# RG-LRU branch of a hybrid block: activations ordered by function over the four column blocks

## Chip, core and metric

The kernel runs on one core of a Trainium2 chip. The metric is device time in microseconds (us) of one execution. The engines are named as the profile names them: PE (matrix products; PEld is its loading of weights), DVE (vector), ACT (scalar engine, which evaluates activation functions from a table that it has to load), POOL and SP (which mostly issue transfers here). Each engine works through its own instructions in program order and waits at an instruction whose inputs are not ready.

## What is computed

A transformer-like block over 256 tokens of width 2048: one wide input projection, four branches in parallel (RG-LRU, attention with a forget gate, Mamba-2, RWKV-7), gates and an output projection, a gated feed-forward part and a last gated addition. All of it is fp32. The part that the change touches is the RG-LRU branch, 512 columns wide:

```python
def rg_lru_branch(x, gate_x, conv_w, conv_b, w_r, b_r, w_i, b_i, lam):
    xc = causal_dwconv(x, conv_w, conv_b)
    xb = xc.reshape(Bsz, S, LRU_BLOCKS, LRU_BLOCK)
    r = sigmoid(einsum('bshi,hij->bshj', xb, w_r) + b_r)
    i = sigmoid(einsum('bshi,hij->bshj', xb, w_i) + b_i)
    log_a = -LRU_C * r * softplus(-lam)
    a = exp(log_a)
    u = xc * i * sqrt(-expm1(2.0 * log_a))
    hseq = associative_scan(combine, (a, u))     # h[t] = a[t] * h[t-1] + u[t]
    return hseq * gelu(gate_x)
```

## The kernel before

Activations lie transposed: features on 128 partitions, 256 tokens along the free axis, so the 512 columns of the branch are four tiles of 128x256, the four blocks `j`.

**The large products** (`gemm_fm`). Weights stream from HBM in chunks of 512 KB (`wr`, four buffers), four feature blocks deep and 256 columns wide. Each chunk is split in two fp32r parts: ACT writes the rounded part (`wh`, L214, three buffers), DVE the remainder (`wl`, L215, three buffers). A unit of 256 output columns is four chunks, each used by 16 matmuls: per feature block and per half of the columns one 128x512 with `wh` and one 128x256 with `wl`. Its two accumulators (`pg`) are two of the four PSUM banks of the pool `psG`. After the last matmul ACT copies one half of the bank (L256) and DVE adds the other (L257, shown as L100, the line of the helper), then DVE multiplies by `R`. Only then is the bank free. Banks are handed out in turn; the small logits' product takes a single one, so from there on a unit gets the second bank of one earlier unit and the first of the next: in the changed kernel's numbers `pg_1002` gets the bank of `pg_719`, `pg_1003` that of `pg_720`, `pg_1106` that of `pg_876`.

**The branches** are Python generators (`lru`, `ssd`, `fox`, `rwkv`). After each chunk a `pump` advances the oldest one to its next `yield`, so that small pieces of branch work lie between the chunks of the large products. Matmuls of a branch (`pb`, pool `psB`) are put into PE's order a little behind the large products' current place (`on_pe`, `DELAY`). From these priorities the framework's scheduler then sets one fixed order for each engine; it places the table loads of ACT too.

**The RG-LRU generator** (`lru`, L523) runs during the projections of `z` and the first `xbc` units, some 60 to 145 us into the execution. For each block: the convolution (ACT an Identity with scale and bias, DVE three multiply-adds, L120), one product each for `r` and `i` with a block-diagonal weight into a `pb` bank, two Sigmoids and a Tanh on ACT, a reciprocal on DVE (L124) and a Sqrt on ACT, four small DVE steps, the scan, a Gelu of the gate column `ag`, and a multiplication. Block 0 goes through all of it before block 1 starts. ACT's functions fall in four tables here: Sigmoid with Tanh, Sqrt, Gelu, and the Silu that the `z` columns need in the same stretch.

Of the kernel before, what the change touches and what calls it, by code (L numbers as in the profile page):

```python
# [10 lines left out]
AF = mybir.ActivationFunctionType  # L11
# [74 lines left out]
def body(tc, T, out, dbg=None):  # L86
# [5 lines left out]
    def shape_n(ap):  # L92
        n = 1
        for s in ap.shape[1:]:
            n *= s
        return n

    def tt(o, a, b, op):
        cost[0] += 0.07 + shape_n(o) / 960.0
        V.tensor_tensor(o, a, b, op=op)  # L100

    def mul(o, a, b):
        tt(o, a, b, ALU.mult)
# [7 lines left out]
    def ts(o, a, s1, s2=None, op0=ALU.mult, op1=ALU.add):  # L111
        cost[0] += 0.07 + shape_n(o) / 1500.0
        if s2 is None:
            V.tensor_scalar(o, a, s1, None, op0=op0)
        else:
            V.tensor_scalar(o, a, s1, s2, op0=op0, op1=op1)
# [5 lines left out]
    def recip(o, a):  # L122
        cost[0] += 0.07 + 8 * shape_n(o) / 960.0
        V.reciprocal(o, a)  # L124

    def act(o, i, f, **kw):
        A.activation(o, i, f, **kw)  # L127
# [10 lines left out]
    def mm(o, l, r, start=True, stop=True):  # L138
        on_pe(PE.matmul, o, l, r, start=start, stop=stop)
# [28 lines left out]
    def slot(dt=F32, pool=sp):  # L168
        return pool.tile([P, S], dt, name="sb" if pool is not sp else "s", tag="s")

    def bank():
        return psB.tile([P, 512], F32, name="pb", tag="pb")
# [9 lines left out]
    def bslot(dt=F32):  # L182
        return slot(dt, bp)
# [166 lines left out]
    def softplus(y, o, w):  # L350

        e, z, z2, q, r = w
        act(e, y, AF.Abs)
        act(e, e, AF.Exp, scale=-1.0)
        ts(r, e, 2.0, None, ALU.add)
        recip(z, r)
        mul(z, z, e)
        mul(z2, z, z)
        ts(q, z2, 1.0 / 17)
        for k in range(7, 0, -1):  # L360
            stt(q, q, 1.0 / (2 * k + 1), z2, ALU.add, ALU.mult)
        stt(q, q, 1.0, z, ALU.add, ALU.mult)
        ts(r, y, 0.0, None, ALU.max)
        stt(o, q, 2.0, r, ALU.mult, ALU.add)
# [35 lines left out]
    raw = {"ax": []}  # L400
# [80 lines left out]
    def pc(name, i):  # L481
        return prm[:, po[name] + i:po[name] + i + 1]
# [24 lines left out]
    def finish(j, tiles):  # L507
        ys[j] = tiles
# [6 lines left out]
    def conv4(x, o, wname, nt, i, bias):  # L515
        if bias is not None:
            act(o, x, AF.Identity, scale=pc(wname, 3 * nt + i), bias=bias)
        else:
            ts(o, x, pc(wname, 3 * nt + i))
        for d in range(1, 4):  # L520
            stt(o[:, d:], x[:, :S - d], pc(wname, (3 - d) * nt + i), o[:, d:], ALU.mult, ALU.add)

    def lru():  # L523
        lam = bc_.tile([P, 7, 4], F32, name="lam")
        lo_ = po["lru_lambda"]
        ts(lam[:, 0], prm[:, lo_:lo_ + 4], -1.0)
        softplus(lam[:, 0], lam[:, 6], [lam[:, i] for i in range(1, 6)])
        ts(lam[:, 0], lam[:, 6], 4.0)
        yield
        res = []  # L530
        for j in range(4):
            ax, ag = raw["ax"][j], raw["ag"][j]
            xc = bslot()
            conv4(ax, xc, "lru_conv_w", 4, j, pc("lru_conv_b", j))
            yield
            pt = bank()
            mm(pt[:, :S], lbd[:, 0, j], xc)
            mm(pt[:, S:], lbd[:, 1, j], xc)
            r, i_ = bslot(), bslot()
            act(r, pt[:, :S], AF.Sigmoid, bias=pc("lru_br", j))  # L540
            act(i_, pt[:, S:], AF.Sigmoid, bias=pc("lru_bi", j))
            t = bslot()
            act(t, r, AF.Tanh, scale=lam[:, 0, j:j + 1])
            yield
            q = r
            ts(q, t, 0.5, 0.5, ALU.mult, ALU.add)
            q2 = bslot()
            recip(q2, q)
            act(t, t, AF.Sqrt)
            yield  # L550
            mul(i_, i_, xc)
            mul(t, t, q2)
            ts(q, q2, -1.0, None, ALU.add)
            mul(i_, i_, t)
            yield
            V.tensor_tensor_scan(xc, q, i_, 0.0, op0=ALU.mult, op1=ALU.add)
            cost[0] += 0.6
            act(t, ag, AF.Gelu_apprx_tanh)
            y = bslot()
            mul(y, xc, t)  # L560
            yield
            res.append(y)
            if dbg is not None:
                dbg("ya", j, y)
            yield
        finish(0, res)
# [568 lines left out]
    hook[0] = first_unit  # L1135
    proj("ag", 0, 2)
    launch("a", lru)
    small_logits()
    proj("z", 2, 2)
# [248 lines left out]
```

## Time and profile before

| | |
|---|---|
| median of 3 runs | 1732.07 us (1731.74 to 1732.73) |
| the profiled execution | 1731.33 us, of which the profile's span is 1729.4 us |
| PE busy | 1713.1 us, 99% of the span |
| DVE busy | 1235.8 us, 71% |
| ACT busy | 946.1 us, 55% |
| ACT table loads | 38, 48.8 us in all |

PE's busy share is so high that time can be gained only where PE stands still, some 16 us in the whole span, or where its clock is below full; and time is lost only where a new wait makes it stand still. A table load is an ACT instruction, so it delays whatever ACT does next, among it the `wh` casts and the copies that empty PE's banks.

### The profile page before, as it was taken

Reading aid. Unit: us, or ns where it says so; the run is one execution under the profiler, and the core shown is the slowest. Engines: PE = TensorE matmul, PEld = TensorE weight load, DVE = VectorE, ACT = ScalarE, POOL = GpSimd, SP = SyncE. Lnnn points to the kernel's source line nnn. Section 1 sums busy time; section 2 is a strip of 40 time slices with the busy share of each in tenths; the row PEclk is TensorE's granted clock in tenths of the full one; section 3 lists DMA queues with packets and bytes.
Section 4 is the critical chain, followed back from the end, with each engine's and each line's share of the span. In section 5 each row is a group of like instructions: output and inputs, shape, how many; then the busy total and the mean of one; then the engine's idle time right before and its main releaser. Section 6 shows DMA issues by size and latency. Waiting matters only on the chain.

```text
span 1729.4 us, 29615 instructions
## 1 busy us (share of the span) xinstructions
PE 1713.1 (99%) x11555; PEld 1558.2 (90%) x11555; DVE 1235.8 (71%) x2006; ACT 946.1 (55%) x1426; POOL 92.6 (5%) x155
## 2 busy tenths in 40 slices
PE   8999999999999999999999999999999999999998
PEld 7888888999999999999888888888888888888887
DVE  6888768687789744648778777777777755555676
ACT  6676555556644444545556555555555544444454
POOL 1000000002320100000210000000000000000000
PEclk9999999999999999999999999999999999999999
DMA  9556556556775854665766666666656666666564
GB/s 330 172 170 217 170 175 225 184 179 206 207 213 178 256 159 150 180 185 189 249 209 192 186 193 187 191 189 189 192 188 202 211 208 189 195 193 186 179 217 139
DMA packets 99132, 338.36 MB, mean 196 GB/s; under 512 B 12362, under 2 KB 16624, under 8 KB 98736
## 3 DMA queue, kind: packets, MB, share of 16 engines
q1 hardware_dynamic: 90528, 310.94, 57.6%
q0 software_dynamic: 7456, 21.81, 4.3%
q10 hardware_dynamic: 1008, 3.73, 0.5%
q8 instruction: 90, 1.47, 0.3%
q14 instruction: 50, 0.41, 0.1%
HBM read 326.95 MB, written 9.48 MB: 195 GB/s over the span
## 4 chain that ended last, share of the span: by engine, by line
PE 94%; DVE 2%; DMA 2%; issue 1%; ACT 1%; SPq 0%; DVEq 0%; ACTq 0%
PE pg L132 90%; PE pb L135 4%; DVE wl L215 1%; PE pb L132 1%; DMA wr<-in_w_p_dram 1%; DMA cbr<-in_consts_dram 0%; DVE e L100 0%; DMA d<-in_xT_dram 0%; ACT wh L214 0%; DVE e L930 0%; DMA wr<-in_w_ax_dram 0%; DVE s L100 0%; ACT e L127 0%; DVE sb L100 0%; DVE s L120 0%
## 5 line engine op out<-in xcount | busy, mean ns | idle before, releaser
L132 PE MATMUL pg<-x,wh 128*128 128x512 f32 (+1 forms) x4384 | 1170.9, 339 | 5.5 <-DVE sb L100 5.3
L215 DVE TENSOR_TENSOR wl<-wr,wh 128x1024 fp32r<-128x1024 f32 (+1 forms) x592 | 715.5, 1210 | 408.1 <-ACT wh L214 400.5
L214 ACT CAST wh<-wr 128x1024 fp32r<-128x1024 f32 (+1 forms) x592 | 615.7, 1041 | 648.0 <-PE pg L132 495.9
L132 PE MATMUL pg<-x,wl 128*128 128x256 f32 (+1 forms) x3344 | 918.3, 282 | 3.4 <-DVE wl L215 3.4
L132 PEld LDWEIGHTS pg<-x,wh 128*128 128x128 f32 x4384 | 746.7, 188 | 91.2 <-DVE sb L100 3.1
L132 PEld LDWEIGHTS pg<-x,wl 128*128 128x128 f32 (+1 forms) x3344 | 628.8, 188 | 17.4 <-DVE wl L215 5.4
L132 PE MATMUL pg<-f,wh 128*128 128x512 f32 x704 | 243.2, 390 | 0.0
L132 PE MATMUL pg<-f,wl 128*128 128x256 f32 x704 | 195.8, 282 | 0.0
L132 PEld LDWEIGHTS pg<-f,wh 128*128 128x128 f32 x704 | 131.7, 188 | 26.9
L132 PEld LDWEIGHTS pg<-f,wl 128*128 128x128 f32 x704 | 133.0, 189 | 1.0
L132 PE MATMUL pg<-sb,wh 128*128 128x256 f32 x512 | 94.7, 283 | 0.0
L120 DVE SCALAR_TENSOR_TENSOR s<-s,prm 128x255 f32<-128x255 f32 (+1 forms) x176 | 84.1, 478 | 1.7 <-ACT s L127 1.0
L132 PEld LDWEIGHTS pg<-sb,wh 128*128 128x128 f32 x512 | 79.2, 188 | 0.1
L256 ACT COPY s<-pg 128x256 f32<-128x256 f32 x136 | 49.7, 366 | 45.8 <-PE pg L132 45.8
L132 PE MATMUL pg<-sb,wl 128*128 128x256 f32 x256 | 72.5, 284 | 0.0
L100 DVE TENSOR_TENSOR s<-s 128x256 f32<-128x256 f32 (+1 forms) x172 | 70.5, 419 | 1.6 <-ACT s L127 0.4
L127 ACT ACTIVATE s<-s 128x256 f32<-128x256 f32 x140 | 56.6, 413 | 14.9 <-DVE s L100 14.5
L100 DVE TENSOR_TENSOR s<-s,pg 128x256 f32<-128x256 f32 x136 | 56.1, 414 | 8.3 <-ACT s L256 6.6
L127 ACT ACTIVATE s<-s,prm 128x256 f32<-128x256 f32 x88 | 52.4, 596 | 0.7 <-DVE s L100 0.7
L127 ACT ACT_TABLE_LOAD x38 | 48.8, 1283 | 1.8 <-PEq L1378 1.2
L132 PEld LDWEIGHTS pg<-sb,wl 128*128 128x128 f32 x256 | 48.0, 188 | 0.2
L132 PE MATMUL pg<-d,wh 128*128 128x512 f32 x128 | 45.2, 395 | 0.0
(235 smaller groups left out, 1152.3 us busy)
## 6 DMA issues: line engine op xcount, KB each, us to landing
wr<-in_w_up_dram SPq DMA_DIRECT2D x176, 512.0 KB, 4.2
wr<-in_w_g_dram SPq DMA_DIRECT2D x128, 512.0 KB, 3.6
wr<-in_w_down_dram SPq DMA_DIRECT2D x88, 512.0 KB, 4.0
wr<-in_w_p_dram SPq DMA_DIRECT2D x76, 512.0 KB, 3.7
wr<-in_w_branch_dram SPq DMA_DIRECT2D x32, 512.0 KB, 3.7
wr<-in_w_out_dram SPq DMA_DIRECT2D x32, 512.0 KB, 3.8
wr<-in_w_ple_gate_dram SPq DMA_DIRECT2D x32, 512.0 KB, 4.2
wr<-in_w_v_dram SPq DMA_DIRECT2D x8, 512.0 KB, 4.4
```

Of the source, the lines that this page charges most:

```text
L100: V.tensor_tensor(o, a, b, op=op)
L120: V.scalar_tensor_tensor(o, a, s, b, op0=op0, op1=op1)
L127: A.activation(o, i, f, **kw)
L132: return f(*a, **kw)
L135: f(*a, **kw)
L214: A.copy(wh, wr)
L215: V.tensor_tensor(wl, wr, wh.bitcast(F32), op=ALU.subtract)
L256: A.copy(o, pt[:, S:])
```

## The change

The first loop now does the Gelus of all four gate columns in place, at the start of the generator. The second loop goes through convolution, products, Sigmoids, Tanh and `q` for the four blocks and keeps the tiles. A third loop does reciprocal, Sqrt, the small steps, the scan and the final multiplication for the four blocks. The number of yields is the same.

```diff
         ts(lam[:, 0], lam[:, 6], 4.0)
         yield
-        res = []
+        res, kept = [], []
         for j in range(4):
-            ax, ag = raw["ax"][j], raw["ag"][j]
+            act(raw["ag"][j], raw["ag"][j], AF.Gelu_apprx_tanh)
+        for j in range(4):
+            ax = raw["ax"][j]
             xc = bslot()
             conv4(ax, xc, "lru_conv_w", 4, j, pc("lru_conv_b", j))
             yield
...
             q = r
             ts(q, t, 0.5, 0.5, ALU.mult, ALU.add)
+            kept.append((xc, i_, t, q))
+        for j, (xc, i_, t, q) in enumerate(kept):
             q2 = bslot()
             recip(q2, q)
             act(t, t, AF.Sqrt)
...
             V.tensor_tensor_scan(xc, q, i_, 0.0, op0=ALU.mult, op1=ALU.add)
             cost[0] += 0.6
-            act(t, ag, AF.Gelu_apprx_tanh)
-            y = bslot()
-            mul(y, xc, t)
+            y = raw["ag"][j]
+            mul(y, xc, y)
             yield
```

What the scheduler makes of it, first on ACT. The four Gelus stand together behind one table load, but the Sigmoids and Sqrts of the blocks still alternate: ACT's order holds 35 table loads against 38. In the names, `pb` is a block's product, `pg` a bank of a large product, `wh` the rounded weights, `prm` and `lam` parameters.

**First place: the second unit of `z` has just been multiplied.** ACT before, from the Sqrt of block 0 on (`pg_719` and `pg_720` are the first unit of `z`):

```order
L127 ACT_TABLE_LOAD
L127 ACTIVATE sb_797<-sb_797 128x256
L256 COPY sb_847<-pg_719 128x256
L256 COPY sb_851<-pg_720 128x256
L214 CAST wh_1001<-wr_999 128x1024
```

ACT now, from the same Sqrt on:

```order
L127 ACTIVATE sb_801<-sb_801 128x256
L214 CAST wh_1028<-wr_1026 128x1024
L214 CAST wh_1054<-wr_1052 128x1024
L127 ACT_TABLE_LOAD
L127 ACTIVATE sb_848<-pb_845,prm_384 128x256
L127 ACTIVATE sb_849<-pb_845,prm_384 128x256
L127 ACTIVATE sb_852<-sb_848,lam_735 128x256
L127 ACTIVATE sb_863<-sb_368,prm_384 128x256
L256 COPY sb_868<-pg_719 128x256
L256 COPY sb_872<-pg_720 128x256
```

The copies that empty the first unit's banks stood right behind block 0's Sqrt; now they stand behind two `wh` casts, a table load and block 1's Sigmoids, which read block 1's product `pb_845`.

PE at the end of that second unit, before:

```order
L132 MATMUL pg_856<-x_336,wl_934 128x256
L132 MATMUL pg_856<-x_336,wh_933 128x512
L132 MATMUL pg_856<-x_339,wl_934 128x256
L132 MATMUL pg_856<-x_339,wh_933 128x512
L132 MATMUL pg_966<-x_119,wh_970 128x512
```

PE now:

```order
L132 MATMUL pg_877<-x_336,wl_971 128x256
L132 MATMUL pg_877<-x_336,wh_970 128x512
L132 MATMUL pg_877<-x_339,wl_971 128x256
L132 MATMUL pg_877<-x_339,wh_970 128x512
L135 MATMUL pb_845<-sb_818,e_392 128x256 x2
L132 MATMUL pg_1002<-x_119,wh_1006 128x512
```

The product `pb_845` has come between the end of this unit and the first matmul of the next, `pg_1002`, which takes the bank of `pg_719`.

**Second place: one unit later.** ACT before, from block 1's convolution on (`pg_855` and `pg_856` are the second unit of `z`):

```order
L127 ACTIVATE sb_953<-sb_365,prm_384 128x256
L256 COPY sb_958<-pg_855 128x256
L256 COPY sb_962<-pg_856 128x256
L214 CAST wh_1049<-wr_1047 128x1024
L214 CAST wh_1085<-wr_1083 128x1024
```

ACT now, from block 2's Sqrt on (`pg_876` and `pg_877` are that unit):

```order
L127 ACTIVATE sb_907<-sb_907 128x256
L214 CAST wh_1135<-wr_1133 128x1024
L214 CAST wh_1157<-wr_1155 128x1024
L127 ACT_TABLE_LOAD
L127 ACTIVATE sb_962<-pb_959,prm_384 128x256
L127 ACTIVATE sb_963<-pb_959,prm_384 128x256
L127 ACTIVATE sb_966<-sb_962,lam_735 128x256
L256 COPY sb_994<-pg_876 128x256
L256 COPY sb_998<-pg_877 128x256
```

The copies of this unit's banks stand behind block 3's Sigmoids and Tanh, and these behind `wh_1157`, which takes the buffer of `wh_1078`, the last chunk of the unit after.

DVE before, at the additions that empty those banks:

```order
L215 TENSOR_TENSOR wl_1028<-wr_1025,wh_1027 128x1024
L100 TENSOR_TENSOR sb_907<-sb_763,sb_797 128x256
L120 SCALAR_TENSOR_TENSOR sb_953<-sb_365,prm_384,sb_953 128x255
L100 TENSOR_TENSOR sb_958<-sb_958,pg_855 128x256
L100 TENSOR_TENSOR sb_962<-sb_962,pg_856 128x256
```

DVE now:

```order
L215 TENSOR_TENSOR wl_1158<-wr_1155,wh_1157 128x1024
L124 RECIPROCAL sb_983<-sb_797 128x256
L124 RECIPROCAL sb_1130<-sb_848 128x256
L100 TENSOR_TENSOR sb_963<-sb_963,sb_924 128x256
L116 TENSOR_SCALAR sb_962<-sb_966 128x256
L100 TENSOR_TENSOR sb_994<-sb_994,pg_876 128x256
L100 TENSOR_TENSOR sb_998<-sb_998,pg_877 128x256
```

The reciprocals of blocks 0 and 1 stand in one row, behind `wl_1158` and ahead of the addition that empties `pg_876`. On PE, block 3's product `pb_959` stands between the last matmul with `wh_1078` and the first of `pg_1106`, which takes the bank of `pg_876`.

**Third place: the end of the RWKV branch, some 715 us in.** Here DVE scales the branch's output with `d`, which a transfer of POOL's queue brings. DVE before, between two chunks of a large product:

```order
L215 TENSOR_TENSOR wl_8451<-wr_8448,wh_8450 128x1024
L120 SCALAR_TENSOR_TENSOR sb_7878<-sb_7878,stamp_380,d_8084 128x256
L120 SCALAR_TENSOR_TENSOR sb_7899<-sb_7899,stamp_380,d_8084 128x256
L215 TENSOR_TENSOR wl_8489<-wr_8486,wh_8488 128x1024
L120 SCALAR_TENSOR_TENSOR sb_7878<-sb_7878,prm_384,sb_4487 128x256
```

DVE now:

```order
L120 SCALAR_TENSOR_TENSOR sb_7874<-sb_7874,stamp_380,d_8080 128x256
L120 SCALAR_TENSOR_TENSOR sb_7895<-sb_7895,stamp_380,d_8080 128x256
L215 TENSOR_TENSOR wl_8447<-wr_8444,wh_8446 128x1024
L120 SCALAR_TENSOR_TENSOR sb_7874<-sb_7874,prm_384,sb_4483 128x256
L120 SCALAR_TENSOR_TENSOR sb_7895<-sb_7895,prm_384,sb_4785 128x256
```

The two steps that need `d` have moved ahead of `wl_8447`, which PE needs for the large product. Elsewhere the order of PE, ACT and DVE is the same but for a few neighbours, and that of SP's and POOL's queues is unchanged.

## Prediction

> **What bounds the kernel now.** I began with the page's span, its busy times and the chain that ended last:
>
> ```profile
> span 1729.4 us, 29615 instructions
> PE 1713.1 (99%) x11555; PEld 1558.2 (90%) x11555; DVE 1235.8 (71%) x2006; ACT 946.1 (55%) x1426; POOL 92.6 (5%) x155
> PE 94%; DVE 2%; DMA 2%; issue 1%; ACT 1%; SPq 0%; DVEq 0%; ACTq 0%
> ```
>
> PE is the bound. ACT and DVE matter only where they make PE stand still. So next came the waits of PE, first of the whole span, then of the stretch from 76 to 145 us in which the four blocks run (columns: total, times, longest):
>
> ```profile
> PE pg L132 <- DVE sb L100: 5.3, 3, 2.9
> PE pg L132 <- DVE wl L215: 3.4, 6, 1.6
> ...
> PE pg L132 <- DVE sb L100: 1.5, 1, 1.5
> PE pg L132 <- DVE wl L215: 0.2, 1, 0.2
> ```
>
> In that stretch PE loses 1.5 + 0.2 = 1.7 us. The 1.5 shows how it loses them; the timeline around 120 us:
>
> ```profile
> 118.21 1.75 DVE L124 RECIPROCAL sb<-sb 128x256 f32<-128x256 f32 x1
> 118.80 1.28 ACT L127 ACT_TABLE_LOAD   x1
> 119.88 1.16 DVE L215 TENSOR_TENSOR wl<-wr,wh 128x1024 fp32r<-128x1024 f32 x1
> 120.10 0.42 ACT L127 ACTIVATE sb<-sb 128x256 f32<-128x256 f32 x1
> 120.42 0.63 ACT L256 COPY sb<-pg 128x256 f32<-128x256 f32 x2
> 120.96 0.74 DVE L100 TENSOR_TENSOR sb<-sb,pg 128x256 f32<-128x256 f32 x2
> 121.51 0.47 PE L132 MATMUL pg<-x,wh 128*128 128x512 f32 x1 [1.47 <-DVE sb L100]
> ```
>
> A bank of an earlier unit is copied late because a table load and a Sqrt stand ahead of the copy on ACT; DVE's addition follows, then PE may write the bank. Such copies are where this change can gain or lose.
>
> The longest wait of the span, 2.9 us at 708 us, shows a second cost. Windows of it (busy us by engine, then granted PE clock, DMA share, GB/s): the wait, the same length after it, and once more:
>
> ```profile
> 705.30:708.20 2.90, 0.03 (x2) 0.01 (x1) 2.90 (x4) 2.85 (x4) 0.00 (x0) 0.91 0.53 172
> 708.20:711.25 3.05, 3.05 (x15) 3.05 (x15) 2.09 (x6) 2.46 (x5) 0.53 (x1) 0.52 0.57 172
> 711.25:714.30 3.05, 3.05 (x28) 3.05 (x27) 0.00 (x0) 0.73 (x1) 1.75 (x3) 1.00 0.11 22
> ```
>
> After 2.9 us of standing still the granted clock is 0.52 and 15 matmuls run where 28 run at 1.00: 13/28 x 3.05 = 1.4 us more. The 1.5 us wait at 120 us was followed by no such loss; a window right behind it:
>
> ```profile
> 122.00:125.00 3.00, 3.00 (x19) 2.66 (x19) 2.97 (x7) 1.87 (x4) 0.00 (x0) 1.00 0.76 202
> ```
>
> **The change part by part.** *Three table loads fewer.* One is this group's mean:
>
> ```profile
> L127 ACT ACT_TABLE_LOAD x38 | 48.8, 1283 | 1.8 <-PEq L1378 1.2
> ```
>
> 3 x 1.28 = 3.8 us of ACT, which is busy 55%. It moves the end only through PE's waits, so by itself I count nothing: PE's matmuls cover it, and at most the 1.7 us above return. I take these 1.7 us as gone: behind the second place ACT holds one more Sqrt of this branch and no further load for it. The Gelus' load now stands ahead of a `wh` cast near 47 us:
>
> ```profile
> 47.33 1.05 ACT L214 CAST wh<-wr 128x1024 fp32r<-128x1024 f32 x1 [1.08 <-PE pg L132]
> 47.58 2.09 DVE L100 TENSOR_TENSOR sb<-sb,R 128x256 f32<-128x256 f32 x6
> 49.59 1.86 DVE L215 TENSOR_TENSOR wl<-wr,wh 128x1024 fp32r<-128x1024 f32 x2
> ```
>
> The first Gelu waits for the first of these six multiplications (48.0) and ends at 48.4, the cast at 49.45, still before DVE comes to the `wl` at 49.59. Covered: nothing there; without the cover 1.1 us.
>
> [...]
>
> *First place: the bank of `pg_719`.* Rows for the durations:
>
> ```profile
> 75.54 0.39 PE L132 MATMUL pg<-x,wh 128*128 128x512 f32 x1
> 75.89 0.39 PE L132 MATMUL pg<-x,wh 128*128 128x512 f32 x1
> 76.11 1.02 PE L135 MATMUL pb<-sb,e 128*128 128x256 f32 x4
> 76.79 0.47 PE L132 MATMUL pg<-x,wl 128*128 128x256 f32 x1
> 77.64 0.84 ACT L127 ACTIVATE sb<-pb,prm 128x256 f32<-128x256 f32 x2
> 78.36 0.51 ACT L127 ACTIVATE sb<-sb,lam 128x256 f32<-128x256 f32 x1
> 81.69 0.42 ACT L127 ACTIVATE sb<-sb 128x256 f32<-128x256 f32 x1
> 82.02 0.63 ACT L256 COPY sb<-pg 128x256 f32<-128x256 f32 x2
> 89.63 0.59 ACT L127 ACTIVATE sb<-sb,prm 128x256 f32<-128x256 f32 x1
> 90.12 0.62 ACT L256 COPY sb<-pg 128x256 f32<-128x256 f32 x2
> 117.34 0.51 ACT L127 ACTIVATE sb<-sb,lam 128x256 f32<-128x256 f32 x1
> 117.74 1.04 ACT L214 CAST wh<-wr 128x1024 fp32r<-128x1024 f32 x1
> 117.88 0.29 DVE L116 TENSOR_SCALAR sb<-sb 128x256 f32<-128x256 f32 x1
> 126.55 0.48 DVE L120 SCALAR_TENSOR_TENSOR sb<-sb,prm 128x255 f32<-128x255 f32 x1
> ```
>
> Start to start this gives: a pair of matmuls 0.35, a block's product 0.68, Sigmoids 0.72 (77.64 to 78.36), Tanh 0.40, Identity 0.49, Sqrt 0.33.
>
> Before, the copies of `pg_719` and `pg_720` started at 82.02. PE ended the second `z` unit at 76.79 + 21 pairs x 0.35 = 84.1, so it found the bank free. Up to there PE's order is unchanged. Now: the cast `wh_1054` needs the buffer of that unit's last chunk, so it starts at 84.3 and ends at 85.35. Load 1.28: 86.6. Sigmoids 0.72, Tanh 0.40, Identity 0.49: the copy starts at 88.25. On DVE a convolution step (0.48) that waits for the Identity's end (88.35) stands ahead of the addition (0.4): 89.2, and PE follows 0.1 later (121.38 to 121.51 above): 89.3. Without the wait it would go on at 84.1 + 0.68 = 84.8. Loss 4.5 us; if the convolution step is no hindrance 4.2, with the start latencies that I left out 5.
>
> PE's order has 20 matmuls of `pg_1002` before it needs the bank of `pg_720`, emptied 0.3 us after: no second wait.
>
> *Second place: the bank of `pg_876`.* Count from X, when PE has left `wh_1006` and the cast `wh_1078` starts. PE has two blocks' products and 36 matmuls until `pg_1106`: 2 x 0.68 + 18 x 0.35 = 7.7. ACT: cast 1.05, load 1.28, Sigmoids, Tanh and Identity 1.6, cast 1.05, load 1.28, Sqrt 0.33, casts `wh_1135` and `wh_1157` 2.1: X + 8.7. Then ACT still has load, Sigmoids and Tanh before the copy, done at X + 11.5. DVE is later: behind `wl_1158` (1.08 to the next start, 119.88 to 120.96) stand two reciprocals of 1.67 (118.21 to 119.88), a multiplication 0.4, a TENSOR_SCALAR 0.29 and the addition 0.4: X + 14.3, PE at X + 14.4. Loss 6.7 us. Lower end, with DVE no hindrance: 11.5 + 0.5 - 7.7 = 4.3; upper end 7.5.
>
> The chunks behind are not late: `wh_1183` waits for PE itself, 22 matmuls (3.8 us) ahead of its use, and needs 1.05 + 1.2.
>
> *The clock.* Both waits (about 4.2 and 6.4 us standing still) are longer than the 2.9 us after which the clock fell to 0.52. So 1.4 us each, 2.8 together; lower end 0, upper end 2 each.
>
> [...]
>
> *Third place, 715 us.* `wl_8447` now waits behind two steps for `d`:
>
> ```profile
> 714.65 1.23 DVE L215 TENSOR_TENSOR wl<-wr,wh 128x1024 fp32r<-128x1024 f32 x1 [4.30 <-ACT wh L214]
> 715.38 1.05 ACT L214 CAST wh<-wr 128x1024 fp32r<-128x1024 f32 x1 [0.76 <-PE pg L132]
> 716.27 0.88 DVE L120 SCALAR_TENSOR_TENSOR sb<-sb,stamp,d 128x256 f32<-128x256 f32 x2 [0.39 <-DMA d<-rw_gn]
> 717.07 1.22 DVE L215 TENSOR_TENSOR wl<-wr,wh 128x1024 fp32r<-128x1024 f32 x1
> ```
>
> It would end at 717.07 + 1.22 = 718.3 instead of 715.9. The cast at 715.38 was released by PE 29 matmuls before the one that needs `wl_8447`; at 3.05/28 = 0.11 us that is 718.5. Covered by 0.2 us: I count nothing, and up to 1 us if the transfer lands later.
>
> **Sum**, against the profiled execution: 4.5 + 6.7 + 2.8 - 1.7 = +12.3 us, 1731.33 + 12.3 = 1743.6. The median of the runs shown, 1732.07, is 0.74 above that execution, so I forecast 1744.4. PE is busy all through what follows, so nothing gives the time back.
>
> **Rivals.** *The clock stays up:* then 9.5 us, 1741.5. For it: the 1.5 us wait cost no clock; against it: 2.9 us did. *A third wait:* the third place misses its 0.2 us, or a chunk after the waits comes late: 1 to 4 us more, 1747. *Only one place bites*, because ACT runs ahead of my count: +7 us, 1739. *The loads do not matter:* PE arrives so late at both banks that the copies are done, which needs 4.5 and 6.7 us more cover than I find: -1.7, 1730.4, no change that can be told. *Faster:* the branch's loads are worth their length on PE's path: 3.8 us, 1728.2. It decides where PE's waits shrink by more than 3.5 us; against it, only 1.7 us of waits stand in this stretch.
>
> That the change does not do what it says is half the case already: Sigmoids and Sqrts still alternate on ACT, which is why only three loads go.
>
> **How the numbers follow.** The forecast's case 0.60, clock up 0.12, third wait 0.12, one place 0.06, no matter 0.07, faster 0.03. With 0.2% (3.5 us, about what a measurement tells here): faster 0.03, same 0.07, slower 0.90. The forecast's own bounds are 4.2 + 4.3 + 1.4 - 1.7 = 8 to 5 + 7.5 + 4 - 1.7 = 15 us, 1740 to 1747; the range reaches from the one-place rival to the third wait, 1739 to 1748.
>
> **What would show it.** In the profile after: a wait of PE for the addition of about 4 us at 85 us, one of about 6.5 us near 100 us, each followed by some 3 us at a clock near 0.5; none at 120 us; table loads x35. Wrong if PE shows no wait over 2 us between 80 and 110 us.

## The result and the profile after

| | median | lowest to highest, runs |
|---|---|---|
| before | 1732.4 us | 1731.74 to 1732.79, 4 |
| after | 1745.05 us | 1744.16 to 1746.1, 4 |

The ratio is 1.0077, 95% interval 1.0065 to 1.0089: 12.65 us slower. The profiled execution took 1744.16 us, 12.8 us more than that of before. The page of after, its span, busy times, the chain by engine and the table loads:

```profile
span 1742.2 us, 29604 instructions
PE 1717.1 (99%) x11555; PEld 1561.8 (90%) x11555; DVE 1236.3 (71%) x2006; ACT 942.8 (54%) x1423; POOL 92.5 (5%) x155
PE 95%; DVE 2%; ACT 1%; issue 1%; DMA 0%; DVEq 0%; SPq 0%
L127 ACT ACT_TABLE_LOAD x35 | 44.9, 1283 | 1.8 <-PEq L1381 1.2
```

PE is still the bound with the same 11555 matmuls, and ACT has its three loads less (48.8 to 44.9 us) and 3.3 us less busy time. Nothing of this shows why the kernel is slower; PE's waits do. First those of the whole span, then those of 76 to 145 us:

```profile
PE pg L132 <- DVE sb L100: 14.5, 4, 6.4
PE pg L132 <- DVE wl L215: 3.5, 2, 2.6
...
PE pg L132 <- DVE sb L100: 10.6, 2, 6.4
```

The waits for the addition that empties a bank have grown from 5.3 to 14.5 us, and in the blocks' stretch two waits of 10.6 us stand where 1.7 us stood. Is all of the loss there? Windows of before and, behind it, of after that hold the same part of the program (busy us and count by engine, PE's clock, DMA share, GB/s):

```profile
76.00:133.00 57.00, 55.31 (x314) 48.30 (x313) 46.37 (x75) 44.77 (x63) 0.00 (x0) 1.00 0.54 171
...
76.00:146.00 70.00, 59.38 (x319) 51.62 (x318) 50.91 (x84) 45.17 (x64) 0.00 (x0) 0.93 0.46 143
```

57 us became 70 for nearly the same work (319 matmuls against 314). Measured between the same two matmuls, from block 0's product at 76.11 (76.55 in after) to a product at 150.35 (162.82), the stretch takes 12.0 us longer; of the 0.8 us that are left of the 12.8, 0.4 lie ahead of it and the rest behind. In the windows PE is busy only 4 us longer, at a clock of 0.93; the other 9 us are standing still. The first place, in the timeline of after:

```profile
84.69 1.03 PE L135 MATMUL pb<-sb,e 128*128 128x256 f32 x4
84.89 1.04 ACT L214 CAST wh<-wr 128x1024 fp32r<-128x1024 f32 x1 [1.06 <-PE pg L132]
85.95 1.28 ACT L127 ACT_TABLE_LOAD   x1
87.25 0.84 ACT L127 ACTIVATE sb<-pb,prm 128x256 f32<-128x256 f32 x2
87.98 0.51 ACT L127 ACTIVATE sb<-sb,lam 128x256 f32<-128x256 f32 x1
88.38 0.59 ACT L127 ACTIVATE sb<-sb,prm 128x256 f32<-128x256 f32 x1
88.87 0.64 ACT L256 COPY sb<-pg 128x256 f32<-128x256 f32 x2
89.41 0.74 DVE L100 TENSOR_TENSOR sb<-sb,pg 128x256 f32<-128x256 f32 x2
89.96 0.48 PE L132 MATMUL pg<-x,wh 128*128 128x512 f32 x1 [4.25 <-DVE sb L100]
```

This is the row of the forecast: cast, load, Sigmoids, Tanh, Identity, and only then the copies; PE stands still for 4.25 us. The second place, with the long row on DVE:

```profile
103.59 1.02 PE L135 MATMUL pb<-sb,e 128*128 128x256 f32 x4
104.41 2.36 DVE L215 TENSOR_TENSOR wl<-wr,wh 128x1024 fp32r<-128x1024 f32 x2 [1.05 <-ACT wh L214]
106.69 3.36 DVE L124 RECIPROCAL sb<-sb 128x256 f32<-128x256 f32 x2
107.77 1.19 ACT L256 COPY sb<-pg 128x256 f32<-128x256 f32 x4
109.96 0.36 DVE L100 TENSOR_TENSOR sb<-sb 128x256 f32<-128x256 f32 x1
110.24 0.28 DVE L116 TENSOR_SCALAR sb<-sb 128x256 f32<-128x256 f32 x1
110.44 1.40 DVE L100 TENSOR_TENSOR sb<-sb,pg 128x256 f32<-128x256 f32 x4
110.99 0.76 PE L132 MATMUL pg<-x,wh 128*128 128x512 f32 x1 [6.38 <-DVE sb L100]
```

The copies start at 107.77, but DVE adds only after both reciprocals, at 110.44. Behind each place the clock falls (windows of after):

```profile
89.96:93.00 3.04, 3.04 (x12) 2.60 (x13) 1.65 (x5) 3.00 (x5) 0.00 (x0) 0.61 0.10 36
93.00:96.00 3.00, 3.00 (x16) 2.59 (x16) 0.00 (x0) 0.27 (x1) 0.00 (x0) 0.82 0.00 0
96.00:99.00 3.00, 3.00 (x18) 2.65 (x17) 1.23 (x1) 2.30 (x2) 0.00 (x0) 1.00 0.00 0
...
110.99:114.00 3.01, 3.01 (x10) 2.62 (x11) 3.01 (x11) 2.00 (x3) 0.00 (x0) 0.50 0.00 0
```

10 to 12 matmuls run where 18 run at 1.00. The third place, where DVE waits for `d` and PE doesn't wait for DVE:

```profile
729.37 0.88 DVE L120 SCALAR_TENSOR_TENSOR sb<-sb,stamp,d 128x256 f32<-128x256 f32 x2 [5.82 <-DMA d<-rw_gn]
```

### The profile page after: what moved, and what is told of

Read it like the earlier page. It is cut to its first block, busy times and chain, and to the rows that moved or that the text cites. A ratio compares the mean times of both kernels' runs of the same rounds, so it can differ in the third digit from the quotient of the medians.

```text
span 1742.2 us, 29604 instructions
## 1 busy us (share of the span) xinstructions
PE 1717.1 (99%) x11555; PEld 1561.8 (90%) x11555; DVE 1236.3 (71%) x2006; ACT 942.8 (54%) x1423; POOL 92.5 (5%) x155
## 3 DMA queue, kind: packets, MB, share of 16 engines
q8 instruction: 90, 1.47, 0.3%
## 4 chain that ended last, share of the span: by engine, by line
PE 95%; DVE 2%; ACT 1%; issue 1%; DMA 0%; DVEq 0%; SPq 0%
PE pg L132 91%; PE pb L135 3%; PE pb L132 1%; DVE wl L215 1%; ACT wh L214 0%; DMA d<-in_xT_dram 0%; DVE e L100 0%; ACT L127 0%; DVE e L933 0%; ACT sb L127 0%; DVE s L100 0%; DMA wr<-in_w_ax_dram 0%; DVE sb L100 0%; DVE sb L124 0%; DVE sb L120 0%
## 5 line engine op out<-in xcount | busy, mean ns | idle before, releaser
L132 PE MATMUL pg<-x,wh 128*128 128x512 f32 (+1 forms) x4384 | 1173.9, 340 | 14.7 <-DVE sb L100 14.5
L127 ACT ACTIVATE s<-s 128x256 f32<-128x256 f32 x140 | 56.6, 412 | 14.9 <-DVE s L100 14.5
L127 ACT ACT_TABLE_LOAD x35 | 44.9, 1283 | 1.8 <-PEq L1381 1.2
```

The lines of the kernel that those rows point to most:

```text
L132: return f(*a, **kw)
```

## The experiments

Two questions were open. Why do the copies now stand behind the next block's Sigmoids: because of the order by function, or because of something else that the edit carries along? And is the fall of the clock a cost of its own? One thing that the edit moves is not visible in the diff: the helper `recip` also books a charge, `cost[0] += 0.07 + 8 * shape_n(o) / 960.0`, here 2.2 us. `pump` pays a generator 0.5 per half chunk (`RATE`) and does not advance it while the credit is used up. Before, each block paid for its reciprocal ahead of the next block's convolution; in the changed kernel all four pay in the third loop. The other steps behind the Tanh have moved there with their charges as well: of a block's six yields two are left in the second loop. So the blocks' products follow each other faster on PE: they stand 43, 29 and 37 instructions apart in PE's order, where they stood 105, 111 and 87 apart.

**The split alone.** From the changed kernel, the Gelus put back where they were:

```diff
-        for j in range(4):
-            act(raw["ag"][j], raw["ag"][j], AF.Gelu_apprx_tanh)
...
-            y = raw["ag"][j]
-            mul(y, xc, y)
+            act(t, raw["ag"][j], AF.Gelu_apprx_tanh)
+            y = bslot()
+            mul(y, xc, t)
```

> The Gelus stay beside the final multiplications; only roots and scans stand in a third loop. Theory (the copies that empty the banks stand behind the next block's Sigmoids, because the blocks' steps now follow each other faster): the split carries the whole loss. The products of the four blocks stand in PE's order at the same distances as in the changed kernel (43, 29 and 37 instructions), so PE waits about 4.2 us near 85 us and about 5.2 us near 102 us, together 9.4 against 10.6, clock drops of some 2.3 us behind them: 1744.5 us. Rival (the early Gelus in place do the harm, by what they put ahead of the casts or by holding their tiles): about 1732.

Measured: 1745.75 us, ratio 1.0075 (1.006 to 1.009). PE's waits in 76 to 145 us:

```profile
PE pg L132 <- DVE sb L100: 9.0, 2, 4.8
PE pg L132 <- DVE wl L215: 0.2, 1, 0.2
```

The split carries the loss; the early Gelus do not.

**The Gelus alone.** From the kernel before:

```diff
+        for j in range(4):
+            act(raw["ag"][j], raw["ag"][j], AF.Gelu_apprx_tanh)
...
-            act(t, ag, AF.Gelu_apprx_tanh)
-            y = bslot()
-            mul(y, xc, t)
+            y = ag
+            mul(y, xc, y)
```

> Only the Gelus are moved to the start, in place; each block still goes through roots and scan before the next. Theory: no wait of PE for a bank in 76 to 145 us, the 1.5 us wait of the kernel before is gone too: 1731 us, 0.1% under the kernel before, 34 table loads. Rival (early Gelus do the harm): 1744. Rival (a table load is worth its 1.28 us on the path): four loads fewer, 1727.

Measured: 1730.85 us, ratio 0.9991 (0.9982 to 1.0). No wait of PE is left in 76 to 145 us. Four loads fewer, 5.1 us of ACT, bring at most the 1.5 us of the wait that one of them caused.

**Only the charge moved.** This is the changed kernel, with every operation where the change wrote it:

```diff
             ts(q, t, 0.5, 0.5, ALU.mult, ALU.add)
+            cost[0] += 0.07 + 8 * S / 960.0
             kept.append((xc, i_, t, q))
...
-            recip(q2, q)
+            V.reciprocal(q2, q)
```

> The changed kernel with every operation where it is written; only the planner's charge for the reciprocal (0.07 + 8 x 256 / 960 = 2.2 us of credit, of which each half chunk of the large product brings 0.5) is booked in the second loop, where the kernel before booked it, and no longer in the third. Table loads stay 35. Theory (pace): the products of the blocks move to 55, 55 and 47 instructions from each other on PE, the next block's Sigmoids no longer stand ahead of the copies at the unit's end; PE waits at most 0.7 us near 95 us: 1731.4 us, the whole loss gone. Rival (the order by function itself costs: roots and scans late, more tiles held, reciprocals ahead of additions): 1744 to 1745, as the changed kernel.

**Only the instruction moved.** The counterpart:

```diff
+            q2 = bslot()
+            V.reciprocal(q2, q)
-            kept.append((xc, i_, t, q))
+            kept.append((xc, i_, t, q, q2))
...
-            recip(q2, q)
+            cost[0] += 0.07 + 8 * S / 960.0
```

> The counterpart: the reciprocal itself is issued in the second loop as before the change, but its charge stays in the third loop. Theory (pace): the blocks' products stay at the changed kernel's distances (43, 27 and 39), so PE still waits: about 2.0 and 4.2 us around 84 to 90 us (for the convolution on DVE ahead of block 1's product, then for the bank) and about 4.0 and 3.8 us around 103 to 112 us; 14 us of waits and 2 to 4 us of clock: 1748 us, between 1744 and 1750. Rival (the two reciprocals in a row ahead of the addition make the loss of the second place): that place shrinks from 6.4 to about 4 us, and the time to about 1742.

Measured: with the charge moved 1731.82 us, ratio 1.0001 (0.9991 to 1.001); with the instruction moved 1750.01 us, ratio 1.0099 (1.0084 to 1.0114). PE's waits in 76 to 145 us, first with the charge moved, then with the instruction moved:

```profile
PE pg L132 <- ACT wh L214: 0.5, 1, 0.5
...
PE pg L132 <- DVE sb L100: 8.3, 2, 4.5
PE pb L135 <- DVE sb L120: 5.7, 2, 3.8
```

This pair decides between pace and order by function. A number in the planner's books, with no operation moved in the text, takes away the whole loss, and the order by function stays. Taking the two reciprocals out of the second place without it doesn't help: that wait shrinks from 6.4 to 3.9 us, but block 3's product, which waits for its convolution on DVE, now waits 3.8 us itself, and block 1's 1.9.

With the charge back in the second loop, block 1's product comes 12 instructions after the first matmul of `z`'s third unit instead of ahead of it, and the copies of `pg_719` stand ahead of its Sigmoids. The distances of the products on PE become 55, 55 and 47, only some 10 to 26 more than in the changed kernel and far from the 105, 111 and 87 of before. So the charge is a small part of what pulled the blocks together; it is enough because it takes the products of blocks 1 and 3 off the ends of the units.

**Instruction and charge moved together**, so that only Sqrt, small steps and scan stay in the third loop (`recip(q2, q)` ahead of `kept.append`):

> The changed kernel with the reciprocal issued and charged in the second loop: only Sqrt, small steps and scan stay in the third. Theory (pace): the products stand 87, 63 and 65 instructions apart; three waits for banks remain, about 1.8, 1.5 and 1.1 us near 97, 110 and 124 us, none long enough for the clock; the waits at 708 us and behind go: 1731.1 us. Rival (split of roots from Sigmoids costs by itself): 1742 or more.

Measured: 1733.03 us, ratio 1.0007 (0.9998 to 1.0016), 1.9 us over the forecast though well under the rival. The products stand 87, 63 and 65 apart, further than with the charge alone, and still three waits are there. So it is not the distance by itself that decides, but what stands ahead of the copies when a unit ends: at the first of these waits a table load, a Sqrt and an Identity (95.87 to 97.98 us on ACT). The waits in 76 to 145 us came as forecast but for 0.3 us:

```profile
PE pg L132 <- DVE sb L100: 4.7, 3, 2.0
```

The forecast had no loss by the clock behind these waits, and in the profiled execution there is one. Windows of the first of the three waits and of what follows it, 3.41 us each:

```profile
96.89:100.30 3.41, 1.45 (x8) 1.13 (x8) 3.41 (x8) 3.38 (x7) 0.00 (x0) 1.00 0.36 83
100.30:103.72 3.42, 3.42 (x13) 2.84 (x12) 3.39 (x8) 1.38 (x3) 0.00 (x0) 0.50 0.69 220
103.72:107.13 3.41, 3.41 (x22) 3.05 (x21) 1.03 (x2) 1.67 (x2) 0.00 (x0) 1.00 0.03 12
```

A wait of 1.96 us, from 97.11 to 99.07, brought the clock down to 0.50 for 3.42 us: 13 matmuls where 22 run at 1.00, about 1.4 us. That belongs to this execution, with 1735.03 us the longest of ten. Four of the ten have a mean granted clock of 1.000 over the execution, which such a fall would bring to 0.999, and took 1729.98, 1732.45, 1732.77 and 1733.16 us. So the clock does not explain the 1.9 us of the median. Waits outside the stretch add up to about that size (1.0 us at 303 us, which the kernel before doesn't have, and 0.9 us in 700 to 760 us, where the forecast had none left); no run shows that they are the reason.

**The clock by itself.** The changed kernel with products that nobody reads in place of PE's standing still:

```diff
             mm(pt[:, S:], lbd[:, 1, j], xc)
+            if j in (1, 3):
+                idle = bank()
+                for _ in range({1: 11, 3: 16}[j]):
+                    mm(idle[:, :S], lbd[:, 0, j], xc)
```

> The changed kernel, with products that nobody reads put behind the block's own product of blocks 1 and 3 (11 and 16 of 128x256 in fp32, 0.34 us each by the rows, 3.7 and 5.4 us), so that PE works through most of the two waits instead of standing still. Theory (after a wait PE runs some 3 us at about half clock): PE's waits shrink to about 0.5 and 0.9 us, the granted clock stays at 1.00 behind them, and where the changed kernel loses some 2.5 us by the clock nothing is lost: 1741.3 us (1.2 us of the gain come from a slightly different order, the rest from the clock). Rival (the clock drop costs nothing on the path): 1743.8 us.

Measured: 1740.86 us, ratio 1.0057 (1.0045 to 1.007) against 1.0077 for the changed kernel. The fillers cover both waits wholly and even end some 0.2 us late, so nothing was gained at the waits themselves: 18 products in a row (2 of the block, 16 fillers) take 109.92 - 102.34 = 7.58 us, 0.42 each, where the expectation had reckoned 0.34. Windows from 84 us on, after first, then with the fillers:

```profile
84.00:100.00 16.00, 11.75 (x57) 9.93 (x56) 6.92 (x13) 11.58 (x18) 0.00 (x0) 0.89 0.28 89
100.00:124.00 24.00, 17.62 (x91) 15.17 (x90) 19.61 (x35) 16.15 (x24) 0.00 (x0) 0.86 0.40 121
...
84.00:100.00 16.00, 16.00 (x86) 14.07 (x86) 9.55 (x18) 14.87 (x23) 0.00 (x0) 1.00 0.34 105
100.00:124.00 24.00, 24.00 (x131) 21.17 (x130) 19.61 (x33) 14.18 (x22) 0.00 (x0) 1.00 0.42 137
```

The clock now stays at 1.00. What that is worth is read between points that both programs pass with the same matmuls. From the first matmul behind the first place to block 3's product, and from the first matmul behind the second place to the copy of that unit's first bank, in the timelines of after and then of the fillers:

```profile
89.96 0.48 PE L132 MATMUL pg<-x,wh 128*128 128x512 f32 x1 [4.25 <-DVE sb L100]
122.64 0.37 ACT L256 COPY sb<-pg 128x256 f32<-128x256 f32 x1 [0.34 <-PE pg L132]
...
90.16 0.58 PE L132 MATMUL pg<-x,wh 128*128 128x512 f32 x1
102.34 7.93 PE L135 MATMUL pb<-sb,e 128*128 128x256 f32 x36
109.92 0.58 PE L132 MATMUL pg<-x,wh 128*128 128x512 f32 x1
120.04 0.37 ACT L256 COPY sb<-pg 128x256 f32<-128x256 f32 x1 [0.34 <-PE pg L132]
```

103.59 - 89.96 = 13.63 us against 12.18, and 122.64 - 110.99 = 11.65 against 10.12: 1.45 and 1.53, 3.0 us together. The 1.2 us that I had expected from the order didn't come; the clock brought 0.5 more than the 2.5 I had put down. Shown: keeping PE busy with useless work saves about 3 us of the 12.7 (9.3 us above before are left by the medians, 1740.86 to 1731.55).

**Order by function in full**, all products, Sigmoids and Tanh of the four blocks in one step:

```diff
             conv4(ax, xc, "lru_conv_w", 4, j, pc("lru_conv_b", j))
+            kept.append(xc)
             yield
+        convs, kept = kept, []
+        for j, xc in enumerate(convs):
             pt = bank()
...
             act(t, r, AF.Tanh, scale=lam[:, 0, j:j + 1])
-            yield
```

> The change carried out in full: all four convolutions, then in one step without a break the four blocks' products, Sigmoids and Tanh, then the third loop as changed; 33 table loads instead of 35. Theory (pace): no copy stands behind Sigmoids at a unit's end, but the Sigmoids in a row delay two casts: PE waits about 3.1 us near 88 us and 2.6 us near 95 us for a remainder of the weights, some 1 us of clock each at most; the waits at 250 and 708 us go: 1731 to 1733 us. Rival (fewer loads are worth their length): 5 x 1.28 = 6.4 us under the kernel before, 1726.

Measured: 1730.39 us, ratio 0.9995 (0.9985 to 1.0004), with 33 loads. Waits in 76 to 145 us:

```profile
PE pg L132 <- DVE wl L215: 5.0, 2, 2.9
```

Five loads fewer than before, 6.4 us of ACT, and no change in time: 5 us of waits for delayed casts are paid back by the waits at 243 us (the 250 of the expectations) and 708 us, which go because the later branches are advanced at other places. The likely reason is a second part of this edit: it takes four yields out, as the last three versions below do, in which the same waits go. Against the kernel before with four yields fewer, 0.9968 below, the full order at 0.9995 is the slower one. So order by function in full pays on ACT here, 48.8 to 42.3 us of loads, and not in the time.

**A faster version.** If pace is what counts, it can be set on purpose. From the Gelus-first kernel, one of two empty steps at the end of each block left out (four steps in all); then the same edit on the kernel before, and on the changed kernel with the charge moved:

```diff
             mul(y, xc, y)
-            yield
             res.append(y)
```

> Only the Gelus first, and one of the two empty steps at the end of each block left out (four in all), which moves all later branch work four half chunks earlier. Theory (pace): no wait in 76 to 145 us as with the Gelus alone, and the waits of the kernel before at 250 us (0.9) and at 708 us (2.9, with 1.4 of clock behind it) go as well, since the branches' steps there no longer meet a unit's end: 1725.7 us, ratio 0.9963, faster than both kernels. Rival (those two waits belong to RWKV's and SSD's own chains and stay): 1731, as with the Gelus alone.

> The kernel before with one thing changed: one of the two empty steps at the end of each block is left out, four in all; the order of functions in each block stays, Gelus included. Theory (pace, not the order of functions, moved the waits at 250 and 708 us): these two waits go, with the 1.4 us of clock behind the second, and the 1.5 us wait at 120 us stays: 1727 us, ratio 0.997. Rival (the early Gelus made the gain of the fastest kernel so far): 1732.

> The changed kernel's order by function in full, with the reciprocal's charge booked in the second loop and the same four empty steps left out. Theory: order by function costs nothing where the pace is right, and is worth only the one wait of 1.5 us at 120 us that it takes away, less the 0.5 us for a cast near 95 us: 1726.3 us, ratio 0.9967, within 2 us of the kernel with the Gelus first and the same pace (1724.8). Rival (roots and scans late cost something later on): 1730 or more.

| | median | ratio, interval | loads |
|---|---|---|---|
| Gelus first, four steps fewer | 1724.79 us | 0.9962, 0.9949 to 0.9974 | 34 |
| before, four steps fewer | 1727.03 us | 0.9968, 0.9956 to 0.9981 | 38 |
| by function, charge moved, four steps fewer | 1724.92 us | 0.9956, 0.9943 to 0.997 | 35 |

All three beat both kernels, and their intervals overlap. PE's waits from 76 to 1200 us in the second and the third:

```profile
PE pg L132 <- DVE sb L100: 1.5, 1, 1.5
PE pg L132 <- DVE s L100: 1.2, 1, 1.2
...
PE pg L132 <- DVE s L100: 1.3, 1, 1.3
PE pg L132 <- ACT wh L214: 0.5, 1, 0.5
PE pg L132 <- DVE sb L100: 0.3, 1, 0.3
```

The 2.9 us wait at 708 us and the 0.96 us one at 243 us are gone in all three, whatever the order of functions; a wait of 0.2 us at some 560 us has grown to 1.2 or 1.3. That order is worth about 2 us at most (1727.03 to 1724.92), with the 1.5 us wait at 120 us as its visible part.

## Why the prediction was right, step by step

The forecast was 1744.4 us (1739 to 1748), the median 1745.05.

- *First place*: PE at 89.3, a loss of 4.5 us. It came at 89.96, on a time axis that runs about 0.5 us late since a wait at 14 us was 1 us longer in this execution. From the end of the block's product (84.69 + 0.68 = 85.37) that is 4.6 us.
- *Second place*: PE at X + 14.4, a loss of 6.7. X was 96.68, so 110.99 is X + 14.3; from 103.59 + 0.68 = 104.27 it is 6.7. DVE's two reciprocals set it, as reckoned; the copies on ACT would have let PE go on some 2.4 us earlier.
- *Clock*: 1.4 us each by the forecast, 1.45 and 1.53 by the fillers. The first fall began 0.7 us behind the wait, at 90.66 (the windows from 87.24 to 90.66 and on to 94.07 are at 1.00 and 0.50), so it reaches into the second window (0.61 and 0.82). The row that the forecast leant on, a fall after 2.9 us, does not stand behind every such wait: behind the same wait of 2.87 us the clock was 1.00 with the Gelus first and with the charge moved (last section). Behind the two new waits, 4.25 and 6.38 us, it fell, as behind the three other waits over 4 us.
- *The wait at 120 us* is gone, as counted (-1.7 us).
- *Third place*: the steps that need `d` waited 5.82 us for their transfer, and the `wl` behind them started at 730.16; PE doesn't wait there. The margin of 0.2 us held; with one so thin, that was partly luck.
- *Sum*: 4.6 + 6.7 + 3.0 - 1.7 = 12.6 us by the forecast's way of counting. By PE's standing still it is 10.6 - 1.7 + 3.0 = 11.9 us, which meets the 12.0 measured between the same matmuls; so the 12.6 is some 0.6 high, and the rest of the 12.8 between the profiled executions lies outside the stretch.
- *Bounds*: the lower one, 8 us, takes 1.4 us for the clock, although the term's lower end was given as 0; with 0 it is 4.2 + 4.3 - 1.7 = 6.8 us, or 1738.9, just under the range.

Where the prediction fell short is not a term but a cause. It read the two places from the order and did not ask why the products had moved there. It took it for half the case that Sigmoids and Sqrts still alternate; the run by function in full shows that completing the change takes away the loss but brings nothing against the kernel before (0.9995). Nor did the clock fall after every wait of some 2.9 us, as the last section shows.

## What to carry to other kernels

Where a planner paces small work by booked costs, moving an operation moves its charge, and the charge can matter more than the operation, even if it shifts the neighbours by only a few instructions: look at where the neighbours land in each engine's order before asking what the edit saves. When one engine is busy 99% of the span, search for the few places where a result must be emptied before it goes on, and count along each engine's order what stands ahead of that emptying. Fewer table loads were worth no more here than the waits that a load stood in.

## What the runs showed of the hardware

Between 1.96 and 2.94 us, the length of PE's wait did not tell in these traces whether the granted clock falls behind it. Waits of PE, and the clock in the two windows behind each, some 3 us long:

| run | wait of PE | clock behind it |
|---|---|---|
| before, at 120 us | 1.47 us | 1.00, 1.00 |
| instruction and charge moved | 1.61 us; 1.96 us | 1.00, 1.00; 0.71, 0.71 |
| by function in full | 2.06 us; 2.94 us | 0.56, 0.88; 1.00 up to the next wait |
| before, at 708 us | 2.87 us | 0.52, 1.00 |
| after, at 721 us | 2.87 us | 0.62, 0.82 |
| Gelus first | 2.87 us | 1.00, 1.00 |
| charge moved | 2.87 us | 1.00, 1.00 |
| instruction moved | 3.86 us; 4.48 us | 0.50, 0.85; 0.50, 0.88 |
| split alone | 4.25 us; 4.76 us | 0.54, 1.00; 0.50, 0.82 |
| after | 4.25 us; 6.38 us | 0.61, 0.82; 0.50, 0.91 |

Of these, the shortest wait with a fall behind it is 1.96 us, the longest without one 2.94 us; all five over 4 us have one. In the trace of before the clock is at 0.50 from 707.70 to 711.11, 3.41 us. Windows of that length around the 2.87 us wait, before and then with the Gelus alone:

```profile
704.28:707.70 3.42, 1.04 (x9) 0.84 (x7) 3.12 (x3) 2.42 (x3) 0.00 (x0) 1.00 0.51 153
707.70:711.11 3.41, 2.92 (x13) 2.92 (x14) 2.59 (x8) 2.94 (x6) 0.46 (x1) 0.50 0.51 154
...
706.70:710.11 3.41, 1.70 (x14) 1.70 (x15) 3.38 (x8) 3.37 (x5) 0.00 (x0) 1.00 0.47 136
710.11:713.52 3.41, 3.41 (x31) 3.41 (x31) 0.44 (x2) 1.84 (x4) 1.27 (x3) 1.00 0.25 97
```

In the first, PE is busy 1.04 us of the window, so it stands still for 70% of it, and the next window is at 0.50. In the second, PE stands still for 50% of the window that holds the end of the wait, and the next is at 1.00. Windows of that length in the trace of after:

```profile
83.83:87.24 3.41, 1.89 (x10) 1.31 (x9) 2.45 (x2) 2.33 (x3) 0.00 (x0) 1.00 0.62 199
87.24:90.66 3.42, 0.70 (x4) 0.68 (x5) 2.35 (x7) 3.39 (x7) 0.00 (x0) 1.00 0.66 222
90.66:94.07 3.41, 3.41 (x13) 2.82 (x12) 0.95 (x3) 2.57 (x5) 0.00 (x0) 0.50 0.03 8
```

Behind the window in which PE stands still for 45% the clock is at 1.00, behind that of 80% at 0.50; with instruction and charge moved a window of 57% was followed by one at 0.50. Before and with the charge moved, the 2.87 us wait starts at the same 705.32 us, and the clock falls in one of the two traces only. So neither the length of this wait nor its place tells whether it costs the clock; that it is chance rather than a matter of the kernel is my estimate from these four traces. What brings the clock back was not shown.
